# Group A's attention units: a query projection split around the last pattern, one mask per pattern, the missing past handled by zeros, and a store on another queue

## The chip, the cores and the metric

One Trainium2 chip, a program on all 8 NeuronCores, each with 2048 of 16384 tokens and no exchange between cores. The metric is the device time of one execution, as long as its slowest core, in microseconds (us). Some executions fall into a second, slower state in which one die or both run at a lower granted TensorE clock (an execution of e1 took 3302.02 us with 0.926 to 0.933 on cores 0 to 3 and 0.985 to 0.986 on the others; one of e2 took 3570.2 us with 0.842 to 0.908 on all eight); verdicts and comparisons here use fast executions, or the cores of a die that is not disturbed.

## The reference, cut to what matters

```python
# one decoder layer; D_MODEL 2048, SEQ 16384
qa, ka, va, qb, kb, vb = split(x @ w_in + b_in)
qa, ka, qb, kb = rope(...)                      # rotary positions
# group A: 8 heads of 128; keys at distances 0, d, ..., window, for three patterns
A_PATTERNS = ((128, 1), (512, 4), (2048, 16))   # (window, dilation)
#   per head: sum over patterns of exp(scores) @ v, over the sum of all exponentials
# group B: 16 heads of 64, sliding window 128, two kv heads, a sink in the denominator
y = concat(rms_norm(ya), rms_norm(yb)) @ w_out
x = layer_norm(alpha * x + y)
x = layer_norm(alpha * x + swiglu(x))           # D_FF 5632
```

Keys before position 0 do not exist. Only core 0 has such keys: every core computes keys and values for the 2048 tokens before its own as well, and core 0's past is empty.

## The kernel before: the parts that the change and the argument touch

The program is a list of operations per engine, in program order. A helper finds what each operation depends on and puts waits on semaphores in front of it, the newest dependence first:

```python
            for d in sorted(op.deps, reverse=True):      # newest operation first
                ...
                w.append(d)
        ...
            for d in w:                                  # one wait instruction for each semaphore
                dop = self.ops[d]
                key = dop.semkey if dop.is_dma else dop.eng
                need[key] = max(need.get(key, 0), dop.val)
            for key, val in need.items():
                engs[op.eng].wait_ge(...)
```

After the keys and values (to about 515 us) come 32 units of group B and then 32 units of group A (8 heads, 4 residue classes of 512 queries each). In between, every unit also computes one 128 x 512 tile of queries ("projection", 16 matmuls of 512 columns) for a unit 6 places later; the last six units of group A have none left. A unit of group A makes scores, exponentials, masks and value sums for three patterns; the last pattern is the undilated one, with 17 small score matmuls.

```python
    pats = [2, 1, 0]
    for u in range(32):                       # group A
        h, c = u // 4, u % 4
        if c == 0 and h < 7:
            load_kv(h + 1)                    # 8 loads on SyncE for the next head
        ...
        for p_ in range(3):
            nb = 3 * u + p_ + 2               # scores run two patterns ahead
            spend.append(a_S(hn, cn, pats[pn], nb % 2))
            run(dveq, 2 if p_ == 0 else 1)    # rotary operations of the last projection, VectorE
            a_PV(h, c, pats[p_], spend.pop(0), p_ == 0, p_ == 2)
        if u == 0:
            reduce_b(3)                       # last quarter of group B's sum of squares
        a_evac(h, c)                          # output scaling
        proj(u + 32 + LEAD)                   # 16 matmuls

    def a_S(h, c, pat, s):                    # scores on TensorE (cut), then
        S_.act(... Exp(p, sp))                # 128 x 1024 on ScalarE
        ...                                   # masks of patterns 2 and 1: one operation each
        else:                                 # last pattern: 15 blocks of 64 columns, and the two edges
            S_.dve(... tensor_tensor(out=pm, in0=pm, in1=mA1[:, c, 1, None, :].to_broadcast([128, 15, 64])))
            S_.dve(... tensor_tensor(out=pe_, in0=pe_, in1=mA1[:, c, 0, :]))     # 64 columns

    def a_evac(h, c):
        S_.act(ls = Ln(lb)); S_.act(ls = Exp(-ls))      # 1 / denominator
        S_.dve(yc = ob * ls)                            # the output scaling
        S_.act(sq = Square(yc))                         # for the RMS norm (from head 1 on)
        S_.pool(copy yc into the head's output); S_.pool(acc += sq)

    def reduce_b(t):                          # a 128 x 512 f32 reduction matmul, then
        ls, bls = LS[nx("ls", 2)]             # the same ring of two buffers that a_evac uses
        S_.act(ls = Ln(...)); S_.act(ls = Exp(-0.5 ls))
        S_.dma("sp", k.rb_d[:, t * 512:(t + 1) * 512], ls, ...)    # 256 KB store, SyncE's queue
```

The softmax here doesn't subtract the row's maximum and nothing guards it: scores larger than these inputs give would overflow.

## Time and profile before

| | before |
|---|---|
| time, median of the first 3 executions | 3144.35 us (fast ones 3143.33 and 3144.35) |
| span of the profiled execution, slowest core (core 1) | 3145.4 us; the cores lie between 3126.6 and 3145.4 |
| group A, first value matmul of unit 0 to that of unit 3, mean of 8 cores | 34.71 us (32.0 to 37.4) |
| group A, units 3 to 24, mean of 8 cores | 177.66 us (177.5 to 177.8), 8.46 a unit |

From the page of the slowest core: busy time of TensorE, the tenths in 40 slices of the span, and the chain of work that ended last.

```profile
PE 2987.8 (95%) x16117; PEld 1424.9 (45%) x16117; DVE 1088.1 (35%) x1484; ACT 642.4 (20%) x889; POOL 595.6 (19%) x600
PE   5999999998997998999999999999999999999993
PE 78%; DVE 9%; DMA 6%; issue 3%; ACT 2%; POOL 1%; SPq 1%; another core or an unknown queue 0%; DVEq 0%; ACTq 0%; POOLq 0%
```

TensorE is busy nearly everywhere. A slice is 78.6 us; the tenth (from 708 us, 8 tenths) and the thirteenth (from 944 us, 7 tenths) lie in group A. The next view is the list of TensorE's waits in a stretch of group A, core 1, 764 to 956 us: who waited for whom, total us, times, longest.

```profile
PE sp L879 <- DVE arena L837: 10.6, 17, 1.5
PE sp L853 <- issue: 4.4, 6, 0.8
```

L879 is the last pattern's value matmuls, which wait for the 64-column edge mask (L837). L853 is a unit's first value matmuls; "issue" is at the six new heads (0.76 to 0.78 us at those of 798, 832 and 866 us). These waits do not say what sets the period of a unit. The timeline does. Its columns are start in us, duration, engine, line, operation, output<-input, shapes, count and, in brackets, how long the engine had idled and what ended it. One unit of core 1, everything but the main steps of the loop cut:

```profile
847.58 0.70 DVE L902 TENSOR_TENSOR arena<-sp,arena 128x512 bf16<-128x512 f32 x1
848.41 1.37 POOL L915 COPY arena<-arena 128x512 bf16<-128x512 bf16 x1 [6.00 <-DVE arena L902]
848.42 0.63 ACT L910 ACTIVATE arena<-arena 128x512 f32<-128x512 bf16 x1 [2.55 <-DVE arena L902]
848.96 2.12 ACT L826 ACTIVATE arena<-sp 128x1024 bf16<-128x1024 f32 x2
849.59 1.27 POOL L922 TENSOR_TENSOR arena<-arena 128x512 f32<-128x512 f32 x1
850.07 1.30 DVE L835 TENSOR_TENSOR arena<-arena 128x960 bf16<-128x960 bf16 x1 [1.79 <-ACT arena L826]
851.48 0.19 DVE L837 TENSOR_TENSOR arena<-arena 128x64 bf16<-128x64 bf16 x1
851.70 0.75 DVE L319 SCALAR_TENSOR_TENSOR arena<-sp,arena 64x512 f32<-64x512 f32 x1
851.82 0.65 PE L879 MATMUL sp<-arena 128*128 128x32 bf16 x17 [0.54 <-DVE arena L837]
...
855.10 1.06 DVE L328 TENSOR_TENSOR arena<-arena 128x512 bf16<-128x512 f32 x1
856.06 0.70 DVE L902 TENSOR_TENSOR arena<-sp,arena 128x512 bf16<-128x512 f32 x1
```

Read it as a loop: output scaling (L902) -> square (L910) -> exponential (L826) -> mask (L835, L837) -> rotary operations and the next two masks, back to back -> next scaling, 8.48 us later. VectorE idles once, 1.79 us, for the exponential behind the square. TensorE's wait of 0.54 us is slack in another engine's loop.

The first units are different. Core 1 again: a head's loads and the last store of group B's sums (L127 is the helper that issues every DMA) stand on SyncE's queue in this order.

```profile
723.91 15.71 SPq L127 DMA_DIRECT2D arena<-vs  x7
738.26 0.65 PE L820 MATMUL sp<-arena 128*128 128x32 bf16 x17
739.72 1.66 SPq L127 DMA_DIRECT2D rb<-arena  x1
744.31 0.60 ACT L899 ACTIVATE arena<-sp 128x512 f32<-128x512 f32 x1 [9.33 <-DMA rb<-arena]
745.73 0.69 DVE L902 TENSOR_TENSOR arena<-sp,arena 128x512 bf16<-128x512 f32 x1 [7.52 <-ACT arena L900]
746.57 1.01 PE L853 MATMUL sp<-arena 128*128 128x128 bf16 x8 [7.65 <-DVE arena L902]
```

ScalarE's logarithm (L899) waits 9.33 us for a store to leave the buffer that it will write, and TensorE 7.65 us for the scaling behind it.

### The profile page before, as it was taken

What the parts mean: (1) busy time and instruction counts of PE and PEld (TensorE: products, weight loads), DVE (VectorE), ACT (ScalarE), POOL (GpSimd) and SP (SyncE); (2) the same over time, 40 slices, a digit from 0 to 9 for tenths busy, and PEclk for the clock granted to TensorE, in tenths of its full rate; (3) what the DMA queues carried; (4) which work ended last, traced back from release to release, by engine and by line L of the source; (5) the groups of instructions that cost most, each with busy time, mean ns of one, the idle gap of its engine ahead of it and who ended that gap; (6) DMA issues with size and microseconds to landing.
All of it is one profiled execution on the core that took longest, in us unless ns stands there. A gap on an engine that the chain in (4) does not pass through costs nothing.

```text
span 3145.4 us, 40366 instructions; the slowest of 8 cores (3126.6 to 3145.4 us)
## 1 busy us (share of the span) xinstructions
PE 2987.8 (95%) x16117; PEld 1424.9 (45%) x16117; DVE 1088.1 (35%) x1484; ACT 642.4 (20%) x889; POOL 595.6 (19%) x600
## 2 busy tenths in 40 slices
PE   5999999998997998999999999999999999999993
PEld 2445554545664443444444444444444444444441
DVE  0555545886777776421001000002410010100006
ACT  0000001765554133310000001112210000011114
POOL 2000000452332976000000002232000000012231
PEclk8999999999999999999999999999999999999997
DMA  9852214155557787654334445556954434446553
GB/s 171 159 121 77 79 51 83 41 124 126 119 126 193 166 188 171 145 111 81 74 74 81 77 84 133 129 130 146 212 109 80 76 74 79 81 82 106 106 105 110
DMA packets 186568, 352.25 MB, mean 112 GB/s; under 512 B 86288, under 2 KB 104080, under 8 KB 169488
## 3 DMA queue, kind: packets, MB, share of 16 engines
q0 software_dynamic: 31824, 190.63, 34.8%
q1 hardware_dynamic: 136128, 125.50, 14.7%
q10 hardware_dynamic: 18432, 33.56, 3.0%
q8 instruction: 129, 2.11, 0.3%
q14 instruction: 55, 0.45, 0.1%
HBM read 471.50 MB, written 68.75 MB: 172 GB/s over the span
## 4 chain that ended last, share of the span: by engine, by line
PE 78%; DVE 9%; DMA 6%; issue 3%; ACT 2%; POOL 1%; SPq 1%; another core or an unknown queue 0%; DVEq 0%; ACTq 0%; POOLq 0%
PE sp L1247 35%; PE sp L1282 19%; PE sp L468 7%; PE sp L455 7%; PE sp L687 4%; PE sp L1090 3%; DMA arena<-z2s 2%; DMA outT<-arena 2%; DMA arena<-wv 1%; DVE arena L835 1%; DVE arena L1154 1%; DVE arena L1314 1%; DVE arena L1313 1%; ACT arena L826 1%; DVE arena L328 1%
## 5 line engine op out<-in xcount | busy, mean ns | idle before, releaser
L1247 PE MATMUL sp<-arena 128*128 128x512 bf16 x5632 | 1222.5, 380 | 12.4 <-DVE arena L1255 7.3
L1247 PEld LDWEIGHTS sp<-arena 128*128 128x128 bf16 x5632 | 552.2, 98 | 683.9 <-issue 24.0
L1282 PE MATMUL sp<-arena 128*128 128x512 bf16 x2816 | 608.1, 379 | 2.2 <-ACT arena L1254 2.2
L1255 DVE TENSOR_TENSOR arena<-sp,arena 128x512 bf16<-128x512 f32 x176 | 121.7, 692 | 989.6 <-ACT arena L1254 989.6
L1282 PEld LDWEIGHTS sp<-arena 128*128 128x128 bf16 x2816 | 275.4, 98 | 335.0 <-issue 3.2
L1254 ACT ACTIVATE arena<-sp 128x512 f32<-128x512 f32 x176 | 105.0, 597 | 926.1 <-PE sp L1247 919.3
L127 POOL DMA_DIRECT2D arena<-wup x88 | 46.7, 530 | 1114.8 <-PE sp L1247 1076.6
L1289 DVE SCALAR_TENSOR_TENSOR arena<-arena,sp 128x512 f32<-128x512 f32 x64 | 44.0, 688 | 565.0 <-PE sp L1282 308.1
L687 PE MATMUL sp<-arena 128*128 128x512 bf16 x1024 | 231.2, 379 | 4.6 <-DVE arena L346 3.9
L1090 PE MATMUL sp<-arena 128*128 128x512 bf16 x1024 | 222.4, 379 | 5.8 <-DVE arena L1209 3.2
L468 PE MATMUL sp<-arena 128*128 128x512 bf16 x1024 | 222.2, 379 | 0.0
L455 PE MATMUL sp<-arena 128*128 128x384 bf16 (+1 forms) x1168 | 212.2, 344 | 9.1 <-DMA arena<-xT 9.1
L1130 POOL TENSOR_TENSOR arena<-arena 128x512 f32<-128x512 f32 x120 | 158.5, 1321 | 311.6 <-DVE arena L1289 273.6
L455 PEld LDWEIGHTS sp<-arena 128*128 128x128 bf16 x1168 | 114.5, 98 | 105.5 <-issue 12.0
L1131 POOL TENSOR_TENSOR arena<-arena 128x512 f32<-128x512 f32 x120 | 160.2, 1335 | 0.0
L1090 PEld LDWEIGHTS sp<-arena 128*128 128x128 bf16 x1024 | 99.7, 98 | 128.7 <-issue 9.9
L468 PEld LDWEIGHTS sp<-arena 128*128 128x128 bf16 x1024 | 100.2, 98 | 120.3
L687 PEld LDWEIGHTS sp<-arena 128*128 128x128 bf16 x1024 | 97.5, 98 | 120.3 <-issue 8.1
L1129 ACT ACTIVATE arena<-arena 128x512 f32<-128x512 f32 x120 | 75.4, 629 | 339.0 <-DVE arena L1289 243.6
L340 ACT ACTIVATE arena<-sp,arena 128x512 bf16<-128x512 f32 (+1 forms) x37 | 25.1, 679 | 562.2 <-PE sp L488 441.7
L437 DVE TENSOR_TENSOR arena<-sp,arena 128x384 bf16<-128x384 f32 (+1 forms) x81 | 47.7, 605 | 199.6 <-PE sp L455 102.3
L826 ACT ACTIVATE arena<-sp 128x1024 bf16<-128x1024 f32 x96 | 97.5, 1018 | 30.2 <-PE sp L809 11.8
(110 smaller groups left out, 2064.9 us busy)
## 6 DMA issues: line engine op xcount, KB each, us to landing
arena<-wup POOLq DMA_DIRECT2D x88, 1024.0 KB, 7.9
arena<-wdn POOLq DMA_DIRECT2D x32, 1408.0 KB, 11.1
arena<-wout POOLq DMA_DIRECT2D x32, 512.0 KB, 8.5
arena<-xres SPq DMA_DIRECT2D x64, 256.0 KB, 5.9
x1s<-arena ACTq DMA_DIRECT2D x64, 256.0 KB, 5.6
arena<-x1s SPq DMA_DIRECT2D x64, 256.0 KB, 5.1
outT<-arena ACTq DMA_DIRECT2D x64, 256.0 KB, 3.3
arena<-xT POOLq DMA_DIRECT2D x12, 1024.0 KB, 22.0
```

The source lines that it names most:

```text
L455: ins = nc.tensor.matmul(bank(k, bk)[:, 0:c1 - c0], x[:, kc, blk * 128:blk * 128 + 128], wv[:, kc, c0:c1], start=(kc == 0), stop=(kc == KC ...
L468: ins = nc.tensor.matmul(bank(k, bk), wk[h][:, kc, :], x[:, kc, :], start=(kc == 0), stop=(kc == KC - 1))
L687: ins = nc.tensor.matmul(bank(k, bk), w[:, kc, :], x[:, kc, :], start=(kc == 0), stop=(kc == KC - 1))
L826: S_.act(lambda: nc.scalar.activation(out=p, in_=sp[:, :], func=AF.Exp, scale=scA), spb[s], [bp])
L1090: ins = nc.tensor.matmul(bank(k, bk), w[:, kc, :], y[:, kc, hh * 512:(hh + 1) * 512], start=(first and i == 0), stop=(last and i == len(kc ...
L1129: S_.act(lambda: nc.scalar.activation(out=sq, in_=z, func=AF.Square), [bz], [bsq])
L1130: S_.pool(lambda: nc.gpsimd.tensor_tensor(out=za, in0=za, in1=z, op=ALU.add), [bz, bza], [bza])
L1131: S_.pool(lambda: nc.gpsimd.tensor_tensor(out=qa, in0=qa, in1=sq, op=ALU.add), [bsq, bqa], [bqa])
L1247: ins = nc.tensor.matmul(bank(k, a + half), w[:, kc, half * 128:half * 128 + 128], xb[:, kc, hh * 512:(hh + 1) * 512], start=(kc == 0), st ...
L1254: S_.act(lambda si=si, a=a: nc.scalar.activation(out=sg[si][0], in_=bank(k, a), func=AF.Silu), [k.bBK[a]], [sg[si][1]])
L1255: S_.dve(lambda si=si, a=a, f=f, hh=hh: nc.vector.tensor_tensor(out=h[f][:, hh * 512:(hh + 1) * 512], in0=bank(k, a + 1), in1=sg[si][0], o ...
L1282: ins = nc.tensor.matmul(bank(k, bk), w[:, fc, :], h[fc][:, hh * 512:(hh + 1) * 512], start=(fc == 0), stop=(fc == FC - 1))
```

## The change

The intent: fewer and simpler vector operations (one mask per pattern, the same on all cores; core 0's missing past gives zero because its values are zero and its denominators are taken with a matrix of zeros in place of ones), fewer denominator matmuls, and half of the projection as a filler ahead of the last pattern's values. The store of group B's sums moves to ScalarE's queue. Core of the diff:

```diff
-    k.maskA1_d = ein("maskA1", [128, 4, 2, 64])   # and maskA2, maskA3, maskB
+    k.maskA1_d = ein("maskA1", [128, 4, 64])
+    k.mask_d = ein("mask", [128, 3, 256])
+    k.onh_d = ein("onh", [128, 128])              # ones; zeros on core 0
-    k.bv_d = ein("bv", [128, VW])
+    k.bv_d = ein("bv", [2, 128, VW])              # first for the past (zeros on core 0)
...
+    def mask(p, bp, m, b, rows):
+        pg = p.rearrange("p (b f) -> p b f", b=rows)
+        S_.dve(lambda: nc.vector.tensor_tensor(out=pg, in0=pg, in1=m.to_broadcast([128, rows, 1024 // rows]), op=ALU.mult),
+               [bp, b], [bp])
...
-    def proj(tau):
+    def proj(tau, half=None):
...
-            for kc in range(KC):
+            for kc in range(KC) if half is None else range(8 * half, 8 * half + 8):
...
+        if half == 0:
+            return
...
-            pe_, pm = p[:, 0:64], p[:, 64:1024].rearrange("p (b f) -> p b f", b=15)
-            S_.dve(... pm * mA1[:, c, 1] ...)
-            S_.dve(... pe_ * mA1[:, c, 0] ...)
+            mask(p, bp, mA1[:, c, None, :], bmA, 16)
...   # denominators: 4 matmuls (480, 32, 480, 32 columns) become 3 (512, 480, 32); group B 8 become 6
-        S_.dma("sp", k.rb_d[:, t * 512:(t + 1) * 512], ls, ...)
+        S_.dma("act", k.rb_d[:, t * 512:(t + 1) * 512], ls, ...)
...
+            if p_ == 2:
+                proj(u + 32 + LEAD, 0)
             a_PV(h, c, pats[p_], spend.pop(0), p_ == 0, p_ == 2)
...
-        proj(u + 32 + LEAD)
+        proj(u + 32 + LEAD, 1)
```

More of the change, by code (lines that the diff above doesn't have):

```diff
@@ L214, in build @@
     k.ropeBh_d = ein("ropeBh", [128, 2, 128])
-    k.maskA1_d = ein("maskA1", [128, 4, 2, 64])
-    k.maskA2_d = ein("maskA2", [128, 1024])
-    k.maskA3_d = ein("maskA3", [128, 256])
-    k.maskB_d = ein("maskB", [128, 1280])
+    k.maskA1_d = ein("maskA1", [128, 4, 64])
+    k.mask_d = ein("mask", [128, 3, 256])
+    k.onh_d = ein("onh", [128, 128])
     k.perm_d = ein("perm", [128, 128])
@@ L288, in persist @@
     k.ones, k.bones = P("ones", 128)
+    k.onh, k.bonh = P("onh", 128)
     k.onesf, k.bonesf = P("onesf", 128, F32)
@@ L414, in phase1 @@
     bx[0] = bl0
-    S_.dma("sp", bv, k.bv_d, [], [bbv], "bv")
+    S_.dma("sp", bv, k.bv_d[0], [], [bbv], "bv")
     o_rb = XO + 4 * X_SLOT + 44 * 2048 + 2 * 25856 - 16384
@@ L544, in phase1 @@
             flush()
+        if t == 3:
+            S_.dma("sp", bv, k.bv_d[1], [], [bbv], "bv")
         if 3 <= t < 7:
@@ L583, in phase2 @@
     SQ = P("sq2", 512, F32)
-    mA2, bmA2 = P("mA2", 1024)
-    mA3, bmA3 = P("mA3", 256)
-    mB0, bmB0 = P("mB0", 1024)
-    mB1, bmB1 = P("mB1", 256)
+    mk, bmk = P("mk", 768)
+    mk = mk.rearrange("p (a b) -> p a b", a=3)
     vB, bvB = P("vB", NKB * 128)
@@ L598, in phase2 @@
     PB.o += 16384
-    mA1, bmA = PB("mA1", 512)
-    mA1 = mA1.rearrange("p (c e f) -> p c e f", c=4, e=2)
+    mA1, bmA = PB("mA1", 256)
+    mA1 = mA1.rearrange("p (c f) -> p c f", c=4)
     xs, bx = k.xs, k.bx
@@ L647, in phase2 @@
         load_wq(i)
-    S_.dma("pool", mB0, k.maskB_d[:, 0:1024], [], [bmB0], "mB0")
-    S_.dma("pool", mB1, k.maskB_d[:, 1024:1280], [], [bmB1], "mB1")
+    S_.dma("pool", mk, k.mask_d, [], [bmk], "mk")
+    S_.dma("pool", k.onh, k.onh_d, [], [k.bonh], "onh")
     S_.dma("pool", mA1, k.maskA1_d, [], [bmA], "mA1")
-    S_.dma("pool", mA2, k.maskA2_d, [], [bmA2], "mA2")
-    S_.dma("pool", mA3, k.maskA3_d, [], [bmA3], "mA3")
+    def mask(p, bp, m, b, rows):
+        pg = p.rearrange("p (b f) -> p b f", b=rows)
+        S_.dve(lambda: nc.vector.tensor_tensor(out=pg, in0=pg, in1=m.to_broadcast([128, rows, 1024 // rows]), op=ALU.mult),
+               [bp, b], [bp])
     ct = {"pj": 0, "t": 0, "p": 0, "ls": 0, "yc": 0}
@@ L675, in proj @@
         ci, tt = tau // 4, tau % 4
-        if tt == 0:
+        if tt == 0 and half != 1:
             if ci >= 1:
                 load_wq(ci + 2)
-        if tt == 0 and ci == 7:
-            S_.dma("sp", ra, k.ropeA_d[4:8].rearrange("t p a b -> p t a b"), [], [bra], "raq")
+            if ci == 7:
+                S_.dma("sp", ra, k.ropeA_d[4:8].rearrange("t p a b -> p t a b"), [], [bra], "raq")
         w, bw = wcur[ci]
-        bk = 6 + nx("pj", 2)
+        bk = 6 + tau % 2
         x = xs[tt]
         def mm():
-            for kc in range(KC):
+            for kc in range(KC) if half is None else range(8 * half, 8 * half + 8):
                 ins = nc.tensor.matmul(bank(k, bk), w[:, kc, :], x[:, kc, :], start=(kc == 0), stop=(kc == KC - 1))
@@ L712, in b_blocks @@
     def b_blocks(kq):
-        return [(4 * kq + 3, 0, 384, 128), (4 * kq - 1, 128, 0, 128)] + [(4 * kq + i, 256 + 256 * i, 128 * i, 256) for i in range(3)]
+        return [(4 * kq + i, 256 * i, 128 * i, 256) for i in range(3)] + [(4 * kq + 3, 768, 384, 128), (4 * kq - 1, 896, 0, 128)]
     def b_S(j, kq):
@@ L732, in b_S @@
             S_.act(lambda e=e, p=p: nc.scalar.activation(out=p, in_=k.SP[e][:, :], func=AF.Exp, scale=scB), spb[e], [bp])
-            if kq == 0:
-                S_.dve(lambda p=p: nc.vector.tensor_tensor(out=p, in0=p, in1=mB0, op=ALU.mult), [bp, bmB0], [bp])
-            else:
-                p4 = p.rearrange("p (b f) -> p b f", b=4)
-                S_.dve(lambda p4=p4: nc.vector.tensor_tensor(out=p4, in0=p4, in1=mB1[:, None, :].to_broadcast([128, 4, 256]),
-                                                             op=ALU.mult), [bp, bmB1], [bp])
+            mask(p, bp, mk[:, 2, None, :], bmk, 4)
             res.append((p, bp))
@@ L751, in mm @@
                     st[e] = False
-            st = [True, True]
-            for part in range(4):
+            for part in range(3):
                 for e in range(2):
-                    p = ps[e][0]
-                    p3 = p[:, 256:1024].rearrange("p (b n) -> p b n", b=3)
+                    p4 = ps[e][0].rearrange("p (b n) -> p b n", b=4)
+                    w = k.ones
+                    lo = lb[64 * e:64 * e + 64]
                     if part == 0:
-                        r, o_ = p3[:, :, 0:128], lb[64 * e:64 * e + 64, 0:384]
+                        r, o_ = p4[:, :, 0:128], lo
                     elif part == 1:
-                        r, o_ = p[:, 0:128], lb[64 * e:64 * e + 64, 384:512]
-                    elif part == 2:
-                        r, o_ = p3[:, :, 128:256], lb[64 * e:64 * e + 64, 128:512]
-                    else:
-                        r, o_ = p[:, 128:256], lb[64 * e:64 * e + 64, 0:128]
-                    ins = nc.tensor.matmul(o_, k.ones[:, 0:64], r, start=st[e], stop=(part == 3), skip_group_check=True)
-                    st[e] = False
+                        r, o_ = p4[:, 0:3, 128:256], lo[:, 128:512]
+                    else:
+                        r, o_ = p4[:, 3, 128:256], lo[:, 0:128]
+                        w = k.onh if kq == 0 else k.ones
+                    ins = nc.tensor.matmul(o_, w[:, 0:64], r, start=(part == 0), stop=(part == 2), skip_group_check=True)
             return ins
-        S_.pe(mm, [ps[0][1], ps[1][1], bvB, k.bones], [bOB, bLB])
+        S_.pe(mm, [ps[0][1], ps[1][1], bvB, k.bones, k.bonh], [bOB, bLB])
     def sq_acc(first, t, src, bsrc):
@@ L793, in b_evac, with groups @@
             k.bys[8 + j] = b
-    cols1 = [(-1, 0, 32), (15, 32, 32)] + [(kb, 64 + 64 * kb, 64) for kb in range(15)]
-    cols2 = [(-1, 0, 128), (3, 128, 128)] + [(j, 256 + 256 * j, 256) for j in range(3)]
+    def groups(n, w):
+        return [(b, b, 0, 2 * w, w * b) for b in range(n - 1)] + [(n - 1, n - 1, 0, w, w * (n - 1)), (-1, n - 1, w, w, 0)]
     def a_S(h, c, pat, s):
@@ L811, in mm @@
             elif pat == 1:
-                for (j, co, n) in cols2:
-                    m0 = 0 if j == -1 else 32 * j
+                s4 = sp.rearrange("p (g a m) -> p g a m", g=4, a=4)
+                for (j, g, mo, n, m0) in groups(4, 32):
                     kc_ = kt[:, (4 + j) * 512:(5 + j) * 512].rearrange("p (i c) -> p c i", c=4)[:, c]
-                    ins = nc.tensor.matmul(sp[:, co:co + n].rearrange("p (a m) -> p a m", a=4), kc_,
-                                           qc[:, :, m0:m0 + n // 4], start=True, stop=True, skip_group_check=True)
-            else:
-                for (kb, co, n) in cols1:
-                    m0 = 0 if kb == -1 else 8 * kb
-                    ins = nc.tensor.matmul(sp[:, co:co + n].rearrange("p (a m) -> p a m", a=4),
-                                           kt[:, 2048 + 128 * kb:2176 + 128 * kb],
-                                           qc[:, :, m0:m0 + n // 4], start=True, stop=True, skip_group_check=True)
+                    ins = nc.tensor.matmul(s4[:, g, :, mo:mo + n], kc_, qc[:, :, m0:m0 + n], start=True, stop=True, skip_group_check=True)
+            else:
+                s4 = sp.rearrange("p (g a m) -> p g a m", g=16, a=4)
+                for (kb, g, mo, n, m0) in groups(16, 8):
+                    ins = nc.tensor.matmul(s4[:, g, :, mo:mo + n], kt[:, 2048 + 128 * kb:2176 + 128 * kb], qc[:, :, m0:m0 + n],
+                                           start=True, stop=True, skip_group_check=True)
             return ins
@@ L826, in a_S @@
         S_.act(lambda: nc.scalar.activation(out=p, in_=sp[:, :], func=AF.Exp, scale=scA), spb[s], [bp])
-        if pat == 2:
-            p4 = p.rearrange("p (a f) -> p a f", a=4)
-            S_.dve(lambda: nc.vector.tensor_tensor(out=p4, in0=p4, in1=mA3[:, None, :].to_broadcast([128, 4, 256]), op=ALU.mult),
-                   [bp, bmA3], [bp])
-        elif pat == 1:
-            S_.dve(lambda: nc.vector.tensor_tensor(out=p, in0=p, in1=mA2, op=ALU.mult), [bp, bmA2], [bp])
-        else:
-            pe_, pm = p[:, 0:64], p[:, 64:1024].rearrange("p (b f) -> p b f", b=15)
-            S_.dve(lambda: nc.vector.tensor_tensor(out=pm, in0=pm, in1=mA1[:, c, 1, None, :].to_broadcast([128, 15, 64]), op=ALU.mult),
-                   [bp, bmA], [bp])
-            S_.dve(lambda: nc.vector.tensor_tensor(out=pe_, in0=pe_, in1=mA1[:, c, 0, :], op=ALU.mult), [bp, bmA], [], [bp])
+        if pat == 0:
+            mask(p, bp, mA1[:, c, None, :], bmA, 16)
+        else:
+            mask(p, bp, mk[:, 2 - pat, None, :], bmk, 4)
         return (p, bp)
@@ L855, in mm @@
                         st = False
-                st = first
                 for f in range(2):
-                    ins = nc.tensor.matmul(l3, k.ones, p4[:, :, f, :], start=st, stop=(last and f == 1), skip_group_check=True)
-                    st = False
-            elif pat == 1:
-                for (j, co, n) in cols2:
-                    m0 = 0 if j == -1 else 32 * j
-                    nc.tensor.matmul(o3[:, :, m0:m0 + n // 4], vt[:, 17 + 5 * c + j + 1, :],
-                                     p[:, co:co + n].rearrange("p (a m) -> p a m", a=4), start=st, stop=False, skip_group_check=True)
-                    st = False
-                st = first
-                pm = p[:, 256:1024].rearrange("p (j a m) -> p j a m", j=3, a=4)
-                for half in range(2):
-                    pe_ = p[:, 128 * (1 - half):128 * (1 - half) + 128].rearrange("p (a m) -> p a m", a=4)
-                    mo = 32 * half
-                    me = 96 if half == 0 else 0
-                    nc.tensor.matmul(l3[:, :, mo:mo + 96].rearrange("p a (j m) -> p j a m", j=3), k.ones, pm[:, :, :, mo:mo + 32],
-                                     start=st, stop=False, skip_group_check=True)
-                    st = False
-                    ins = nc.tensor.matmul(l3[:, :, me:me + 32], k.ones, pe_, start=False, stop=(last and half == 1), skip_group_check=True)
-            else:
-                for (kb, co, n) in cols1:
-                    m0 = 0 if kb == -1 else 8 * kb
-                    nc.tensor.matmul(o3[:, :, m0:m0 + n // 4], vt[:, kb + 1, :],
-                                     p[:, co:co + n].rearrange("p (a m) -> p a m", a=4), start=st, stop=False, skip_group_check=True)
-                    st = False
-                st = first
-                pm = p[:, 64:1024].rearrange("p (b a m) -> p b a m", b=15, a=4)
-                for half in range(2):
-                    pe_ = p[:, 32 * (1 - half):32 * (1 - half) + 32].rearrange("p (a m) -> p a m", a=4)
-                    mo = 8 * half
-                    me = 120 if half == 0 else 0
-                    nc.tensor.matmul(l3[:, :, mo:mo + 120].rearrange("p a (b m) -> p b a m", b=15), k.ones, pm[:, :, :, mo:mo + 8],
-                                     start=st, stop=False, skip_group_check=True)
-                    st = False
-                    ins = nc.tensor.matmul(l3[:, :, me:me + 8], k.ones, pe_, start=False, stop=(last and half == 1), skip_group_check=True)
@@ new lines, in mm @@
+                    ins = nc.tensor.matmul(l3, (k.onh, k.ones)[f], p4[:, :, f, :], start=(first and f == 0), stop=False,
+                                           skip_group_check=True)
+            else:
+                n_, w = (4, 32) if pat == 1 else (16, 8)
+                v0 = 17 + 5 * c if pat == 1 else 0
+                p4 = p.rearrange("p (g a m) -> p g a m", g=n_, a=4)
+                for (b, g, mo, n, m0) in groups(n_, w):
+                    nc.tensor.matmul(o3[:, :, m0:m0 + n], vt[:, v0 + b + 1, :], p4[:, g, :, mo:mo + n], start=st, stop=False,
+                                     skip_group_check=True)
+                    st = False
+                pr = p.rearrange("p (g a m) -> p a g m", g=n_, a=4)
+                nc.tensor.matmul(l3.rearrange("p a (g m) -> p a g m", g=n_), k.ones, pr[:, :, :, 0:w], start=first, stop=False,
+                                 skip_group_check=True)
+                nc.tensor.matmul(l3[:, :, w:128].rearrange("p a (g m) -> p a g m", g=n_ - 1), k.ones, pr[:, :, 0:n_ - 1, w:2 * w],
+                                 start=False, stop=False, skip_group_check=True)
+                ins = nc.tensor.matmul(l3[:, :, 0:w], k.onh, p4[:, n_ - 1, :, w:2 * w], start=False, stop=last, skip_group_check=True)
@@ L892, in mm @@
             return ins
-        S_.pe(mm, [pb[1], bv_, k.bones], [bOB, bLB])
+        S_.pe(mm, [pb[1], bv_, k.bones, k.bonh], [bOB, bLB])
     k.y7 = None
@@ L950, in reduce_b @@
         b = Buf("rb%d" % t)
-        S_.dma("sp", k.rb_d[:, t * 512:(t + 1) * 512], ls, [bls], [b], "rbs%d" % t)
+        S_.dma("act", k.rb_d[:, t * 512:(t + 1) * 512], ls, [bls], [b], "rbs%d" % t)
         rsum.append(b)
@@ L1341, in _masks @@
     z = lambda c: np.where(c, 1.0, 0.0).astype(f)
-    on = 1.0 if core > 0 else 0.0
     p = np.arange(128)
     a = np.arange(4)
-    m1 = np.zeros((128, 4, 2, 64), f)
+    m1 = np.zeros((128, 4, 64), f)
     for c in range(4):
-        def dist(mus):
-            q = (16 * mus[None, :] + 4 * a[:, None] + c).reshape(-1)
-            return q[None, :] - p[:, None]
-        d = dist(np.arange(16))
-        m1[:, c, 1] = z((d >= 0) & (d <= 128))
-        d = dist(np.arange(8, 16))
-        if core > 0:
-            m1[:, c, 0, 0:32] = z((d >= 0) & (d <= 128))
-        d = dist(np.arange(8))
-        m1[:, c, 0, 32:64] = z((d >= 0) & (d <= 128))
-    def d2(ms):
-        q = (4 * ms[None, :] + a[:, None]).reshape(-1)
-        d = q[None, :] - p[:, None]
-        return z((d >= 0) & (d <= 128))
-    m2 = np.zeros((128, 1024), f)
-    if core > 0:
-        m2[:, 0:128] = d2(np.arange(32, 64))
-    m2[:, 128:256] = d2(np.arange(32))
-    for j in range(3):
-        m2[:, 256 + 256 * j:512 + 256 * j] = d2(np.arange(64))
+        q = (16 * np.arange(16)[None, :] + 4 * a[:, None] + c).reshape(-1)
+        d = q[None, :] - p[:, None]
+        m1[:, c] = z((d >= 0) & (d <= 128))
+    q = (4 * np.arange(64)[None, :] + a[:, None]).reshape(-1)
+    d = q[None, :] - p[:, None]
     q = np.arange(128)
     cur = z(q[None, :] >= p[:, None])
-    prevA = z(q[None, :] <= p[:, None])
-    prevB = z(q[None, :] < p[:, None])
-    m3 = np.zeros((128, 256), f)
-    if core > 0:
-        m3[:, 0:128] = prevA
-    m3[:, 128:256] = cur
-    mb = np.zeros((128, 5, 256), f)
-    mb[:, :, 0:128] = cur[:, None]
-    mb[:, :, 128:256] = prevB[:, None]
-    if core == 0:
-        mb[:, 0, 128:256] = 0.0
-    mb = mb.reshape(128, 1280)
-    return dict(maskA1=m1, maskA2=m2, maskA3=m3, maskB=mb)
+    m = np.zeros((128, 3, 256), f)
+    m[:, 1] = z((d >= 0) & (d <= 128))
+    m[:, 0] = np.concatenate([z(q[None, :] <= p[:, None]), cur], 1)
+    m[:, 2] = np.concatenate([cur, z(q[None, :] < p[:, None])], 1)
+    return dict(maskA1=m1, mask=m, onh=np.full((128, 128), 1.0 if core > 0 else 0.0, f))
 def prepare_inputs(x, w_in, b_in, sinks, g_mix_a, g_mix_b, w_out, ln1_g, ln1_b, w_up, w_down, ln2_g, ln2_b):
@@ L1404, in prepare_inputs @@
     bsw = con(np.concatenate([swap(bka), swap(bqa)], 1))
-    bv = con(np.broadcast_to(np.concatenate([b_in[2048:3072], b_in[4224:4352]])[None], (128, VW)))
+    bvt = con(np.broadcast_to(np.concatenate([b_in[2048:3072], b_in[4224:4352]])[None], (128, VW)))
     wout = chunks(w_out)
@@ L1421, in prepare_inputs @@
         pb[i, base + ((i - base) + 32) % 64] = 1.0
-    shared = dict(wq=wq, wk=wk, wkb=wkb, wv=wv, bqk=bqk, bsw=bsw, bv=bv, wout=wout, wup=wup, wdn=wdn, gmix=gmix, lnp=lnp,
+    shared = dict(wq=wq, wk=wk, wkb=wkb, wv=wv, bqk=bqk, bsw=bsw, wout=wout, wup=wup, wdn=wdn, gmix=gmix, lnp=lnp,
                   sinks=sk, perm=pb)
@@ L1437, in prepare_inputs @@
         m.update(_masks(c))
+        m["bv"] = np.stack([bvt if c > 0 else np.zeros_like(bvt), bvt])
         in_maps.append(m)
```

## The prediction

> **What bounds the kernel now.** The page of the slowest core shows TensorE busy 95% of 3145.4 us; the chain of waits puts 78% on it. The change works in the attention stage alone: group B's 32 units (about 515 to 715 us) and group A's 32 (719.8 to about 1001 us). Two places there are not TensorE-bound.
>
> 1. Group A's steady units. In the timeline, units with a projection repeat every 8.48 us, though TensorE waits only 0.55 us in each, before the last pattern's values (view of waits: 11.7 us in 19 waits, on the small edge mask). At a new head it waits 0.77 us elsewhere, and the period is the same. So a loop that TensorE is not in sets it: VectorE's output scaling ends; ScalarE squares the output (0.63) and only then makes the last pattern's exponential (1.02); VectorE, idle 1.79 us until then, does the main mask (1.31 instead of 0.66), the edge mask (0.22 start to start), four rotary operations, two more masks, then the next scaling without a pause. The mask takes double while GpSimd copies and adds (1.38 + 1.28 us right after the scaling)[...].
> 2. Group A's first units. ScalarE waits 9.33 us for a 256 KB store of group B's sums, issued on SyncE behind a head's value loads; TensorE then waits 7.65 us (4.9 to 7.7 over the cores), plus 0.8 to 2.3 us one unit earlier. After it matmuls run near half speed for 4 us (eight in 1.01 instead of 0.61).
>
> **What the change does.**
> - Store to ScalarE's queue: removes the wait in 2. Core 1 takes 36.6 us for the first three units; without waits and slow clock I estimate 0.85 (one reduction) + 3 x 8.2 = 25.5. Worth 11 us on core 1, about 8 on the cores that waited 5.
> - One mask for the last pattern: 0.22 less, 0.04 more for 64 columns: 0.18 us of the loop, in about 28 units: 5 us.
> - Halved projection: 8 x 0.2155 = 1.72 us of matmuls ahead of the last pattern's values hide the 0.55 us wait. But VectorE's loop stays, so TensorE should idle instead after the second half, before the next unit's first values, on the output scaling: 0.3 to 0.6 us a unit. Alone worth nothing. The later denominators leave the logarithm and exponential some 0.4 us of slack.
> - Denominator matmuls 4 to 3 (8 to 6 in group B): the same columns; under 1 us in all.
> - Smaller masks, zero bias and ones: loads off the path, one bias reload of 0.6 MB hidden behind eight key tiles: nothing.
> - The last six units have no projection (waits 1.9 to 3.9 us on the scaling): only the mask's 0.18 each, counted above.
>
> Later stages are TensorE-bound and just start earlier.
>
> **Prediction.** 11 + 5 + 0.5, less on other cores: 3128 us, range 3114 to 3140. Faster by over 2%: 1%; within: 97%; slower: 2%.
>
> **What would show it.** Right: group A's period 8.3 us, VectorE idle only some 1.8 us before the last pattern's mask; the edge-mask wait gone; a new TensorE wait on the output scaling in most units; the 7 us wait gone on all cores. Wrong: a period near 7.9 us (then TensorE bounded it), or VectorE idle before the scaling (then the half-projection delayed the denominators).
>
> **What would make it wrong.** Less GpSimd contention, a slower strided denominator read, the 0.4 us slack used up, or the slow state in the median.

The sum: 11 + 5 + 0.5 us, about 16 from the 3144.35 before to 3128. The 0.5 stands for the denominators ("under 1 us in all"), an estimate that is not worked out from a trace.

## The result, and the profile after

The kernel after took 3138.86 us (median of 4 fast executions, 3137.71 to 3140.38) against 3144.35 us for the kernel before (median of its 3 fast executions, 3143.33 to 3146.27; a fourth was slow, 3522.82). The ratio is 0.9982 with a 95% interval of 0.9962 to 1.0001. Ratios are computed as the mean time of one kernel's fast runs over that of the other's of the same rounds, so they are not quite the ratio of the quoted medians. The gain is 0.2%, 5.7 us, a third of the 16 us that were forecast; the interval just includes no gain at all. The time lies inside the forecast range, but the size of the gain was wrong.

The time of the slowest core hides most of this, for what follows the start of unit 31, the last of group A, takes 2137 to 2152 us before and 2140 to 2153 us after, differing from core to core and from run to run without any change of the code. So I read stages, as means over the eight cores. A unit starts at its first value matmul (eight 128x128 matmuls, L853 before, L846 after).

| stage, us | before | after | difference | forecast |
|---|---|---|---|---|
| start to unit 0 | 719.32 | 719.39 | +0.1 | 0 |
| units 0 to 3 | 34.71 | 28.25 | -6.5 | -8 to -11 |
| units 3 to 24 | 177.66 | 175.88 | -1.8 | -3.8 (21 x 0.18) |
| units 24 to 31 | 59.64 | 59.31 | -0.3 | -1.3 (7 x 0.18) |
| unit 31 to the end | 2145.3 | 2146.4 | +1.1 | 0 |
| whole, mean of the cores | 3136.7 | 3129.2 | -7.4 | |

The same lines of the page as before, of its slowest core (core 6):

```profile
PE 2985.4 (95%) x15989; PEld 1423.7 (45%) x15989; DVE 1086.0 (35%) x1452; ACT 643.2 (21%) x889; POOL 594.4 (19%) x598
PE   5999999999997998999999999999999999999993
PE 81%; DVE 7%; DMA 5%; issue 3%; ACT 2%; POOL 1%; another core or an unknown queue 0%; DVEq 0%; ACTq 0%; SPq 0%; POOLq 0%
```

Busy time of TensorE is the same within 2.4 us; the tenth slice, with group A's first units, went from 8 to 9 tenths. Its waits in the same part of group A, core 1, 755 to 938 us:

```profile
PE sp L846 <- DVE arena L876: 13.5, 18, 1.3
```

The wait for the edge mask is gone and one on the output scaling (L876) has come in its place, of about the same sum, as forecast. The timeline of core 1, the loop of one ordinary unit and then of the first unit of a head:

```profile
846.08 0.71 DVE L876 TENSOR_TENSOR arena<-sp,arena 128x512 bf16<-128x512 f32 x1
846.93 0.61 PE L846 MATMUL sp<-arena 128*128 128x128 bf16 x8 [0.53 <-DVE arena L876]
848.58 1.35 DVE L655 TENSOR_TENSOR arena<-arena 128x1024 bf16<-128x1024 bf16 x1 [1.79 <-ACT arena L826]
852.25 0.18 PE L865 MATMUL sp<-arena 128*128 128x32 bf16 x1
853.22 0.63 ACT L874 ACTIVATE arena<-arena 128x512 f32<-128x512 f32 x1
854.31 0.69 DVE L876 TENSOR_TENSOR arena<-sp,arena 128x512 bf16<-128x512 f32 x1
855.90 0.61 PE L846 MATMUL sp<-arena 128*128 128x128 bf16 x8 [1.25 <-DVE arena L876]
856.80 1.33 DVE L655 TENSOR_TENSOR arena<-arena 128x1024 bf16<-128x1024 bf16 x1 [1.79 <-ACT arena L826]
861.21 0.18 PE L865 MATMUL sp<-arena 128*128 128x32 bf16 x1
862.17 0.63 ACT L874 ACTIVATE arena<-arena 128x512 f32<-128x512 f32 x1
862.91 0.69 DVE L876 TENSOR_TENSOR arena<-sp,arena 128x512 bf16<-128x512 f32 x1 [0.29 <-ACT arena L874]
```

An ordinary unit takes 8.23 us from scaling to scaling (846.08 to 854.31), 0.25 less than the 8.48 before. The first unit of a head takes 8.60 (854.31 to 862.91). There TensorE starts its first values 0.90 us after the scaling's end (855.00) instead of 0.14 us after it (846.79), 0.76 us later, because the waits on the head's loads come behind the wait on the scaling; the denominators come later by as much, and VectorE idles for the exponential of the logarithm (L874), which it did nowhere between 764 and 956 us before. In an ordinary unit that exponential starts 1.09 us before the scaling; at the new head the scaling follows 0.74 us after it, which is what it needs. The slack was 0.35 us, the delay 0.76.

The first units, on core 5, the one with the longest wait that is left:

```profile
719.17 17.47 SPq L127 DMA_DIRECT2D arena<-vs  x7
719.77 0.33 ACTq L127 DMA_DIRECT2D rb<-arena  x1
727.08 0.33 ACTq L127 DMA_DIRECT2D rb<-arena  x1
730.96 0.60 ACT L873 ACTIVATE arena<-sp 128x512 f32<-128x512 f32 x1 [3.95 <-DMA rb<-arena]
733.21 1.01 PE L846 MATMUL sp<-arena 128*128 128x128 bf16 x8 [5.42 <-DVE arena L876]
```

The stores are issued in time now. But the one of the third quarter, issued at 719.77 here, lands 11 us later, beside seven loads of values, and ScalarE waits for its buffer. Before, that store stood ahead of the loads on SyncE's queue and landed within 2.8 to 3.8 us on all cores, and the wait was for the last one, issued behind them; after, it takes 5.0 to 11.1 us. On core 1 the store is not waited for, yet TensorE waits 1.97 us there all the same. So two things remained open: what is left in the first units, and where the mask's gain went.

### The profile page after: what moved, and what is told of

Its sections match the earlier page's. It is cut to its first block, busy times and chain, and to the rows that moved or that the text cites. A ratio compares the mean times of both kernels' runs of the same rounds, so it can differ in the third digit from the quotient of the medians.

```text
span 3137.1 us, 40048 instructions; the slowest of 8 cores (3122.0 to 3137.1 us)
## 1 busy us (share of the span) xinstructions
PE 2985.4 (95%) x15989; PEld 1423.7 (45%) x15989; DVE 1086.0 (35%) x1452; ACT 643.2 (21%) x889; POOL 594.4 (19%) x598
## 4 chain that ended last, share of the span: by engine, by line
PE 81%; DVE 7%; DMA 5%; issue 3%; ACT 2%; POOL 1%; another core or an unknown queue 0%; DVEq 0%; ACTq 0%; SPq 0%; POOLq 0%
PE sp L1223 35%; PE sp L1258 19%; PE sp L468 7%; PE sp L455 7%; PE sp L692 4%; PE sp L1066 4%; DMA arena<-z2s 2%; DMA arena<-wv 1%; DMA outT<-arena 1%; DVE arena L655 1%; DVE arena L1130 1%; DVE arena L1290 1%; DVE arena L1289 1%; DVE arena L876 1%; ACT arena L826 1%
## 5 line engine op out<-in xcount | busy, mean ns | idle before, releaser
L1223 PEld LDWEIGHTS sp<-arena 128*128 128x128 bf16 x5632 | 551.4, 98 | 685.7 <-issue 25.5
L655 DVE TENSOR_TENSOR arena<-arena 128x1024 bf16<-128x1024 bf16 x160 | 144.3, 916 | 65.3 <-ACT arena L826 54.1
L340 ACT ACTIVATE arena<-sp,arena 128x512 bf16<-128x512 f32 (+1 forms) x37 | 25.1, 678 | 564.1 <-PE sp L488 443.6
```

Of the source, the lines that this page charges most:

```text
L655: S_.dve(lambda: nc.vector.tensor_tensor(out=pg, in0=pg, in1=m.to_broadcast([128, rows, 1024 // rows]), op=ALU.mult), [bp, b], [bp])
L1223: ins = nc.tensor.matmul(bank(k, a + half), w[:, kc, half * 128:half * 128 + 128], xb[:, kc, hh * 512:(hh + 1) * 512], start=(kc == 0), st ...
```

## The experiments

Theory: (1) a loop of VectorE and ScalarE sets the unit, so only the single mask shortens it; (2) the split projection moves the denominators later, and with the waits at a new head that costs time; (3) the store's move takes away the queue's part of the first wait only, while landing and ScalarE's order remain. Rivals are named in each expectation. All kernels were correct.

| us, mean of 8 cores | units 0 to 3 | units 3 to 24 | units 24 to 31 |
|---|---|---|---|
| before | 34.71 | 177.66 | 59.64 |
| after | 28.25 | 175.88 | 59.31 |
| e1 store only | 27.21 | 178.30 | 60.56 |
| e2 split only | 34.78 | 179.97 | 60.20 |
| e3 after, projection whole | 27.67 | 172.60 | 59.41 |
| e4 after, oldest waits first | 28.10 | 172.09 | 59.80 |
| e5 after, own buffers for the sums | 27.29 | 175.62 | 59.59 |
| e6 e5 and a later reduction | 25.10 | 175.62 | 60.10 |
| e7 before, late squares | 34.42 | 175.41 | 61.79 |
| e8 after, late squares | 28.34 | 170.51 | 60.99 |
| e9 all, projection whole | 26.04 | 160.23 | 61.40 |
| e10 all, projection split | 25.48 | 165.28 | 60.81 |
| e11 e3 with two masks (cores 0 to 3) | 27.52 | 178.32 | 60.23 |

Each row is one profiled execution. Within a run the eight cores agree on units 3 to 24 to within 0.5 us, and kernels whose edits do not touch these units agree from run to run (after, e5 and e6: 175.6 to 175.9), so differences of 1 us and more there are above the noise, while most whole times are not. Units 0 to 3 differ by up to 6.5 us between the cores of one run, so their means say less. For the whole time, e5 (3134.67 us), e6 (3136.19), e8 (3140.48) and e10 have one fast execution each and e11 none.

### e1: the store alone

```diff
 # kernel before
-        S_.dma("sp", k.rb_d[:, t * 512:(t + 1) * 512], ls, [bls], [b], "rbs%d" % t)
+        S_.dma("act", k.rb_d[:, t * 512:(t + 1) * 512], ls, [bls], [b], "rbs%d" % t)
```

> Kernel before with one edit: the store of group B's sums goes to ScalarE's queue. Stages are read from the trace as means over the eight cores, between the first value matmul of group A's units: units 0 to 3 took 34.7 us before and 28.25 after the change; units 3 to 24 took 177.66 and 175.88. If the store alone makes the gain of the first units: units 0 to 3 about 28.3, units 3 to 24 unchanged at 177.7, whole kernel 6 us faster than before. Rival (the halved projection or the new mask shares in it): units 0 to 3 above 31.

Units 0 to 3 fell to 27.21 us, and units 3 to 24 stayed within 0.64 us (178.30; from the scaling of unit 7 to that of unit 23 it is 135.8 us in both). The whole gain of the first units comes from this line. The whole time gave a ratio of 0.9987 (0.9955 to 1.002): the 6 us can't be seen in it.

### e2: the split projection alone

```diff
 # kernel before
+            if p_ == 2:
+                proj(u + 32 + LEAD, 0)        # matmuls 0 to 7
             a_PV(h, c, pats[p_], spend.pop(0), p_ == 0, p_ == 2)
...
-        proj(u + 32 + LEAD)
+        proj(u + 32 + LEAD, 1)                # matmuls 8 to 15
```

> Kernel before with the halved projection alone. Theory (VectorE and ScalarE's loop sets the period): the wait before the last pattern's values goes, but units 3 to 24 stay at 177.7 to 178.8 us, inside a head 8.47 us a unit, at a new head a little longer than 8.55; units 0 to 3 about 34.7. Rival (the halved projection is what shortened the unit): 8.24 us inside a head and units 3 to 24 at 176 or less.

Units 3 to 24 took 179.97 us, 2.3 more than before and more than the theory allowed at its upper end. The filler that was to take TensorE's wait away makes these units slower when it comes alone. Part of the 2.3 comes from how the first units end: from the scaling of unit 7 to that of unit 23, with four new heads, it is 136.8 us against 135.8. (Whole time: ratio 1.0023, 0.9975 to 1.0071.)

### e3: the kernel after with the projection whole

```diff
 # kernel after
-            if p_ == 2:
-                proj(u + 32 + LEAD, 0)
             a_PV(h, c, pats[p_], spend.pop(0), p_ == 0, p_ == 2)
...
-        proj(u + 32 + LEAD, 1)
+        proj(u + 32 + LEAD)
```

> Kernel after with the projection whole again, at the end of the unit. Theory: 8.24 us inside a head comes from the single mask and stays; at a new head the seven waits on loads (0.76 us) fall into TensorE's slack again, so the 8.6 to 8.9 us of those units go to about 8.3, and units 3 to 24 take 173 to 174 us, 2 us less than after. Rival (the halved projection gives the gain): 8.47 a unit and 177.7.

Units 3 to 24 took 172.60 us, 3.3 less than the kernel after; the theory said 173 to 174. Between e1 (178.30) and e3 lie the masks, the denominators and the zeros, 5.7 us in 21 units. Median 3132.57 us, ratio 0.9958 (0.9936 to 0.9981): undoing the split more than doubles the gain of the change.

### e4: the same waits, the oldest first

```diff
 # kernel after, in the helper that places the waits
-            for d in w:
+            for d in reversed(w):
```

> Kernel after; every engine waits on the same semaphores, but the oldest first, so at a new head TensorE passes the seven waits on the loads while it idles anyway for the output scaling. Theory (these waits, 0.76 us behind the scaling, use up the 0.4 us slack of the logarithm and exponential): units at a new head go from 8.6 to 8.9 down to 8.3 us, units 3 to 24 from 175.9 to 173.3. Rival (something else about a new head, such as the arrival of loads or GpSimd): 175.9 stays.

Units 3 to 24 took 172.09 us. From unit 5 on every unit of core 1 in that range takes 8.20 to 8.25 us, new head or not, and TensorE's waits on the scaling (core 1, 755 to 938 us) are at most 0.5 us:

```profile
PE sp L846 <- DVE arena L876: 11.1, 22, 0.5
```

With this order the split no longer costs anything (172.09 against e3's 172.60). That comparison favours e4 a little: unit 24 is the first of a head, so in e3 its first values stand behind the waits on the loads. From scaling to scaling this falls out, and the result is the same: units 7 to 23 take 131.6 us in e3, 131.6 in e4 and 133.7 in the kernel after, about 0.5 for each of the four new heads; unit 4, the first new head, takes 7.9, 7.9 and 8.7. So the split's price in the kernel after lies in the order of the waits; the waits that count are the seven on a new head's loads, since only the units at a new head changed (the edit reorders the waits of all engines; e3 with this order was not run). The four executions that count as fast lie from 3129.27 to 3159.97 us, two of them with one pair of cores at a slightly lower clock (0.975 to 0.977), too far apart for a verdict on the whole time (ratio 0.9999, 0.9928 to 1.007).

### e5: buffers of their own for the stored sums

```diff
 # kernel after
+    RB = [P("rbs%d" % i, 512, F32) for i in range(2)]
...
-        ls, bls = LS[nx("ls", 2)]             # in reduce_b
+        ls, bls = RB[t % 2]
```

> Kernel after; the stored sums of group B get two buffers of their own, so that no output scaling of group A waits for a store to land. Theory (what is left of the first units' wait is partly the landing of the store, 1 to 4 us on the cores where the loads of the next head are slow): the wait of ScalarE on that store goes on every core, and units 0 to 3 go from 28.25 us in the mean (26.5 to 32.0) to 26.5 on all. Rival (the store is not in it): no change.

ScalarE's wait for the store is gone from core 5, and the cores lie at 26.5 or 28.1 us (mean 27.29) instead of 26.5 to 32.0. That is half of what was expected. The wait of 1.97 us on the scaling stayed on every core. Behind it matmuls of cores 2, 4, 6 and 7 ran near half speed (on core 2 five took 1.01 us instead of 0.60), and those cores took 6.02 to 6.07 us from unit 1's first value matmul to its first of the last pattern; cores 0, 1, 3 and 5 did not slow down and took 4.40 to 4.41, which is the difference between 28.1 and 26.5. In the kernel after, core 1 shows a granted clock of 0.50 at the same place (731.5 to 733.6 us).

### e6: the last reduction behind the first output scaling

```diff
 # kernel e5
-        if u == 0:
-            reduce_b(3)
         a_evac(h, c)
         proj(u + 32 + LEAD, 1)
+        if u == 0:
+            reduce_b(3)
```

> As the run with own buffers, and the last reduction of group B, with its logarithm, exponential and store, comes after the first output scaling of group A in place of before it. Theory (the rest is ScalarE's order: 1.4 us of reduction and 0.8 us of store stand ahead of the first unit's logarithm): the 2 us wait of TensorE before unit 1 goes, and units 0 to 3 take 25 to 25.5 us. Rival: 26.5 stays, the reduction only moves.

25.1 us on every core (25.1 to 25.2). In this kernel the remaining wait was ScalarE's order of work: logarithm, exponential and store of a reduction stood ahead of the logarithm that TensorE waited for. (The store is the small part: in the kernel after it took 0.33 us of ScalarE's queue, and on core 1 the next activation came 0.51 us after the end of the one that made the stored data, 719.28 to 719.79.) The estimate of 25.5 us in the prediction was right for a kernel without these waits; the change did not take them all away.

But the order alone does not make the wait. The same place, unit 1's first values, in the kernel after (core 1) and in e3 (core 0), both without a wait for a store and with the reduction ahead:

```profile
729.35 0.61 PE L846 MATMUL sp<-arena 128*128 128x128 bf16 x8 [1.97 <-DVE arena L876]
728.22 0.61 PE L846 MATMUL sp<-arena 128*128 128x128 bf16 x8 [0.24 <-DVE arena L876]
```

With the projection whole, 16 matmuls and not 8 cover ScalarE's work; units 0 to 3 of e3's core 0 take 24.76 us, and e1 waits as little on cores 1 and 2. So this wait, too, is a price of the split, and e6 is one of two ways to remove it. In e3's other cores the store's landing then shows (2.0 to 4.6 us of ScalarE's wait).

### e7: late squares in the kernel before

```diff
 # kernel before, in a_evac
-            S_.act(lambda: nc.scalar.activation(out=sq, in_=yc, func=AF.Square), [byc], [SQ[1]])
+            lateq.append(lambda: S_.act(lambda: nc.scalar.activation(out=sq, in_=yc, func=AF.Square), [byc], [SQ[1]]))
...  # the sum on GpSimd in the same way; both are run behind the next unit's last-pattern scores:
                 spend.append(a_S(hn, cn, pats[pn], nb % 2))
+            run(lateq, 2)
```

> Kernel before with one edit: the square of a unit's output and its sum are put behind the next unit's last-pattern exponential in program order. If the loop output scaling, square, exponential, mask, rotary operations, next scaling sets the period, it gets 0.63 us shorter at the least, and more if the mask then runs beside less of GpSimd's work, until TensorE bounds the unit at about 7.7 us (its shortest units without any wait): units 3 to 24 from 177.7 to 164 to 168 us. Rival (TensorE and its waits set the period): 177.7 stays, or falls by less than 2 us.

Units 3 to 24 took 175.41 us: only 2.3 less, 8.30 us inside a head, so this expectation failed. By its letter the rival missed too, by 0.3. (Whole time: ratio 0.9995, 0.9973 to 1.0018.) The timeline shows what ate the rest. Core 1, the mask operations and GpSimd's two:

```profile
838.70 1.37 POOL L916 COPY arena<-arena 128x512 bf16<-128x512 bf16 x1 [5.32 <-DVE arena L903]
840.06 0.66 DVE L835 TENSOR_TENSOR arena<-arena 128x960 bf16<-128x960 bf16 x1 [1.56 <-ACT arena L826]
840.62 1.27 POOL L923 TENSOR_TENSOR arena<-arena 128x512 f32<-128x512 f32 x1 [0.56 <-ACT arena L911]
840.83 1.12 DVE L837 TENSOR_TENSOR arena<-arena 128x64 bf16<-128x64 bf16 x1
```

The large mask now falls between GpSimd's two operations and takes 0.66 us instead of 1.30. But the 64-column mask starts while GpSimd adds, takes 1.12 us instead of 0.19, and ends at 841.95, 0.06 us after the addition. In this trace the small mask did not end before GpSimd's addition, and the two masks together took 1.89 us (840.06 to 841.95) where they took 1.60 before (850.07 to 851.67).

### e8: late squares in the kernel after

The same edit on the kernel after.

> Kernel after, with the square and its sum behind the next unit's last-pattern exponential. With late squares in the kernel before, the 64-column edge mask met GpSimd's addition and took 1.12 us instead of 0.19, ending 0.06 us after it, and the unit only fell to 8.30 us. With one mask there is no second mask to be caught: if VectorE is held by GpSimd's work and not by its own, the mask takes 0.7 us, VectorE is no longer the limit, and the unit inside a head falls from 8.24 to 7.8 to 8.0 us (the halved projection leaves TensorE a wait of 0.1 to 0.3 us on the output scaling); units 3 to 24 take 168 to 171 us. Rival (the mask's own length or its strided form is what takes 1.34 us): 8.2 us and 174 or more.

Units 3 to 24 took 170.51 us, and most units inside a head 7.85 us. With one mask there is no second operation to be caught; it took 0.69 us on core 1, against 1.35 in the kernel after, where GpSimd's addition (848.11 to 849.37) ran beside it (848.58 to 849.93). The rival is out: 1.35 us is not the length of the mask in its new form.

### e9 and e10: everything together, with the projection whole and split

One mask, the store on ScalarE's queue, own buffers, the later reduction, the oldest waits first, late squares: e9 with the projection whole, e10 with it split.

> One mask, the store on ScalarE's queue with its own buffers and behind the first output scaling, oldest waits first, late squares, and the projection whole. TensorE should bound the unit: 7.7 us, units 3 to 24 in 162 to 166 us, units 0 to 3 in 24 to 25.5 us, the out-projection's start some 20 to 24 us earlier than in the kernel before, and the whole kernel near 3122 us, 0.7% faster than before and 0.5% faster than after.

> The same with the projection halved. If its price is that the logarithm, exponential and scaling (2.4 us from the last denominator matmul) have only half a projection and one pattern of scores (2.2 us) to hide behind, the unit is 0.1 to 0.4 us longer than with the whole projection: units 3 to 24 at 165 to 170 us. Rival (the halving costs nothing once the loop is short): equal.

e9: units 3 to 24 in 160.23 us, better than expected; units 0 to 3 in 26.04, slightly worse; in units 24 to 31 every kernel with late squares gives some 1.5 to 2 us back. The profile shows no wait of TensorE (of 0.15 us or more) on core 1 between 755 and 920 us, and most units take 7.56 us. Median of its four fast executions 3120.37 us (two more were slow), ratio to before 0.9915 (0.9899 to 0.9931), so this version beats the kernel before clear of the noise; the kernel after was not run beside it, but its four executions (3137.71 to 3140.38) all lie above. The timeline of core 1 shows why the whole projection is better here (L878 is the scaling, L847 the next unit's first values; the first three lines are e9, the last two e10):

```profile
840.24 3.61 PE L693 MATMUL sp<-arena 128*128 128x512 bf16 x16
843.06 0.69 DVE L878 TENSOR_TENSOR arena<-sp,arena 128x512 bf16<-128x512 f32 x1
844.35 0.61 PE L847 MATMUL sp<-arena 128*128 128x128 bf16 x8
844.60 0.69 DVE L878 TENSOR_TENSOR arena<-sp,arena 128x512 bf16<-128x512 f32 x1 [0.75 <-ACT arena L876]
845.43 0.61 PE L847 MATMUL sp<-arena 128*128 128x128 bf16 x8
```

In e9 the scaling is finished 0.6 us before TensorE comes for it. With half a projection to hide behind (e10) it is not: VectorE waits 0.75 us for ScalarE's exponential (L876), and TensorE follows 0.14 us after the scaling's end. Units 3 to 24 take 165.28 us, 5.1 more, 7.85 us a unit. So the split is worth nothing while VectorE's loop is the limit, and costs 0.29 us a unit once TensorE could be it. (e10 was run twice; its one fast execution took 3120.24 us.)

### e11: two masks again

```diff
 # kernel e3
-            mask(p, bp, mA1[:, c, None, :], bmA, 16)
+            pg = p.rearrange("p (b f) -> p b f", b=16)
+            for (r0, r1) in ((0, 15), (15, 16)):          # 960 and 64 columns
+                S_.dve(... pg[:, r0:r1] * mA1[:, c] ...)
```

> Kernel after with the projection whole (which took 172.6 us for units 3 to 24), and the last pattern's mask again in two operations, of 960 and 64 columns, with everything else of the change in place. Theory (the second mask operation, 0.22 us start to start in VectorE's loop, is the whole difference between 8.47 and 8.23 us a unit): units 3 to 24 go to 177 to 178 us. Rival (the new order of columns, the denominators or the ones have a share): they stay below 176 us.

This profile fell in the slow state (die 1 at a clock of 0.956): cores 0 to 3 took 178.3 to 178.4 us for units 3 to 24, a little over the expected 177 to 178 and the same as e1 (178.30) with the old order of columns, the old denominators and the old masks. The second mask operation is the whole difference between e1 and e3. The denominators and the new order are worth nothing that these runs can show.

## Why the prediction was right or wrong

- **What bounds group A: right.** The loop through VectorE and ScalarE sets the unit. TensorE's wait moved from the edge mask to the output scaling with about the same sum, as forecast, and the unit inside a head went to 8.23 us (forecast 8.3).
- **One mask, 0.18 us of the loop, 5 us: right by itself.** Measured 0.25 us a unit and 5.7 us in units 3 to 24 (e1 against e3, e11). But in the change as made only 1.8 us of it arrive there, because of the next point. In the last seven units 0.3 us arrive instead of 1.3; what bounds those I did not look into.
- **"Halved projection ... Alone worth nothing": wrong; this is the step that failed.** It costs 2.3 us alone (e2) and 3.3 us in the change (e3 against after). The prediction had both numbers, 0.77 us of waits at a new head and 0.4 us of slack left for the logarithm and exponential, named the slack as a risk, and did not subtract one from the other. Measured on core 1: slack 0.35 us, delay 0.76, and a unit 0.37 longer at a new head (8.60 against 8.23); over the cores about 0.5 at each of four heads and 0.8 at the first. e4 takes the waits out of the way and the cost with them. The split also brings TensorE's wait of 1.97 us in the first units (e6).
- **The first units, 8 to 11 us: mis-sized.** The store's queue was the right cause (the seven loads of one head hold SyncE's queue for 15.71 us in the kernel before, and taking the store out of it is the 7.5 us of e1), and 25.5 us about the right floor (e6: 25.1), but the change reaches only 28.25: own buffers against the store's landing beside a head's loads bring 1.0 us of the rest (e5), a later reduction on ScalarE 2.2 (e6), which counts because the halved projection no longer covers it. The prediction took for granted that an earlier issue takes every wait away. It does not: the third quarter's store, issued on ScalarE's queue, took 11 us to land on core 5 beside SyncE's loads, and at most 3.8 us on any core ahead of them in the kernel before.
- **Denominators, smaller masks, the bias reload: right**, nothing to be seen; group A starts at the same time within 0.1 us, and the last pattern's denominators take TensorE 0.46 us before (four matmuls, 852.30 to 852.76 on core 1) and 0.44 after (three, 851.84 to 852.28).
- **The sum.** Forecast 16 us; the stages give 8.5 us to the start of unit 31 in the mean of the cores, the spans 7.4, and the slowest core 5.7, since what follows varies by some 15 us between cores. I used the waits of the slowest core for the slowest core's gain; which core is the slowest afterwards is settled in a stage that the change does not touch.

In one account of units 3 to 24, which closes by construction since each term is the difference of two runs: 177.66, store +0.64 (e1), one mask -5.70 (e3; with the denominators and zeros, which e11 shows to be worth nothing here), split +3.28 = 175.88.

## What to carry to other kernels

Before filling an engine's waits, find the loop that sets the period: if the period is the same in units where the engine waits and in units where it does not, the filler only moves the wait. Moving work ahead of a result takes slack from whatever consumes that result, so compare the slack left with every irregular delay on that path, here the waits on a new head's loads (0.76 us against 0.35 us of slack), and pass old waits before new ones (e4). When a wait has a cause in a queue, ask also how long the transfer takes to land under load (here up to 11.1 us in place of 3.8) and what else stands ahead in the waiting engine's own order.
